# Hybrid decoder layer on one core: the last eight weight tiles are kept, and the second half of the tokens ends by column blocks

## The chip, the cores and the metric

The kernel runs on one core of one Trainium2 chip. The metric is the device time of one execution in microseconds. The time before is 1567.35 us, the median of 3 runs (1565.99 to 1568.28). The engines are named as the profile names them: PE is TensorE (matmuls), PEld its weight loads, DVE is VectorE, ACT is ScalarE, POOL is GpSimd and SP is SyncE. A name with q behind it is that engine's queue of issued DMAs.

## The reference

One decoder layer on 256 tokens of 2048 channels, all in float32. Two token mixers share one input projection and one output projection; then comes a gated MLP, and a final norm:

```
mixed = sigmoid(g_a) * y_a + sigmoid(g_b) * y_b
x = x + einsum('bsd,de->bse', mixed, w_out[l])
h = rmsnorm(x, norm_ffn_w[l])
gate, up = split(einsum('bsd,df->bsf', h, w_up[l]), 2, axis=-1)
gate = causal_dwconv(gate, conv_ffn_w[l]) + conv_ffn_b[l]
x = x + einsum('bsf,fd->bsd', gelu(gate) * up, w_down[l])
return rmsnorm(x, norm_final_w)
```

`rmsnorm(x, w)` is `x * rsqrt(mean(x * x) + 1e-6) * w`, one mean for each token. The MLP is 5632 wide, so `w_down` is 5632 x 2048. The change touches only the last two lines: the product with `w_down`, the residual add, the final norm and the write of the result.

## The kernel before

**Matmuls in three parts.** Every matmul of weights is done in a rounded float32 format. A weight tile is split into a high part (the rounded value) and a low part (what rounding left), and so are the activations. A product is three matmuls: high by high, low by high, high by low.

**The weight pipeline.** All weights come as 528 tiles (128 partitions x 1024 values, 512 KB) and two of another shape, in the fixed order of the list `srcs`. `fetch` (line 275) issues the load of a tile `raw` on SyncE's queue, into a ring of 4 buffers. `cast` (284) lets ScalarE write the high part `whi`, `split` (292) lets VectorE write the low part `wlo`, each into a ring of 4 buffers. So a load waits until the split of the tile four places earlier has freed its buffer, and a cast waits until TensorE is done with the tile four places earlier. `weights()` (317) hands out the next pair. A small model of the engines' times (`Plan`, and `pipeline` at 305) decides at which place of the program a fetch, cast or split is written, at most 3 tiles ahead of the one in use; what an engine then waits for, in program order, is settled on the chip.

**The product with `w_down`.** The activations stand in `hhi` and `hlo` (high and low part), the residual stream `x` in the tile `xt`. The result is 256 tokens x 2048 channels. It is accumulated in eight PSUM banks at once: two token halves t = 0, 1 of 128 tokens, by four column blocks c = 0 to 3 of 512 channels. `acc[c][t]` names them: for c = 0 and 1 they are tiles of their own (`psa`, t = 0, and `psb`, t = 1), for c = 2 and 3 both halves lie in one tile of two banks (`psm`). The rows of `w_down` are walked in 22 steps `kp` of 256 rows; each step has four weight tiles, one for each column block. `down_part(kp, c, t, hi, lo)` (1223) issues the six matmuls (two groups of 128 rows, three parts) of one tile for one token half. In the steps before the last, each tile is used for both halves in turn, 12 matmuls. In the last step (`LAST`, 1230) block 0 is done for both halves; then the loop over t takes blocks 1 to 3 of the first half, and ends that half, and then blocks 1 to 3 of the second half, and ends that one.

**How a half ends** (the loop over t, from line 1245). For each block, VectorE adds the PSUM bank to `xt`, and ScalarE squares the sum and sums it up by token (`sqj` is the square's scratch tile, `ssq5` the sums). VectorE reduces the four sums and scales them (`rs`), GpSimd raises to the power -0.5. VectorE multiplies blocks 2 and 3 by the norm's weights `nfin` meanwhile (called weighing below). Then blocks 0 and 1 are scaled and weighed in one VectorE operation, and blocks 2 and 3 are scaled by ScalarE. All four writes of a half are issued on SyncE's queue, in the order 0, 2, 1, 3. `nfin` was loaded in one broadcast load behind step 12, on ScalarE's queue.

Nearly every instruction is recorded through a helper, so the profile gives line 94 for all; they are told apart by their tiles.

Of the kernel before, what the change touches and what calls it, by code (L numbers as in the profile page):

```python
# [13 lines left out]
P = 128  # L14
# [93 lines left out]
def kernel(  # L108
# [35 lines left out]
    def nm(s):  # L144
        cnt[0] += 1
        return f"{s}_{cnt[0]}"
# [125 lines left out]
    def soon(eng, time):  # L272
        return time <= max(now["PE"], now[eng])

    def fetch():
        i = len(raws)
        src = srcs[i]
        raw = wpool.tile(list(src.shape), F32, tag="raw", name=nm("raw"), bufs=4)
        plan.at(free[i - 4] if i >= 4 else 0.0)
        nc.sync.dma_start(raw, src)  # L280
        landed.append(plan.ready)
        raws.append(raw)

    def cast():
        i = len(rounded)
        hi = wpool.tile(list(raws[i].shape), F32R, tag="whi", name=nm("whi"))
        plan.at(max(landed[i], now["PE"] if i > AHEAD else 0.0))
        nc.scalar.copy(hi, raws[i])
        cast_at.append(plan.ready)
        rounded.append(hi)  # L290

    def split():
        i = len(made)
        raw, hi = raws[i], rounded[i]
        plan.at(max(cast_at[i], now["PE"] if i > AHEAD else 0.0))
        if hi.shape[1] == 8:
            lo = None
            nc.vector.tensor_tensor(hi[:, :, 32:64], raw[:, :, 0:32], hi[:, :, 0:32].bitcast(F32), op=ALU.subtract)
        else:
            lo = wpool.tile(list(raw.shape), F32R, tag="wlo", name=nm("wlo"))  # L300
            nc.vector.tensor_tensor(lo, raw, hi.bitcast(F32), op=ALU.subtract)
        free.append(plan.ready)
        made.append((hi, lo))
# [923 lines left out]
            mm(acc[c][t], ll(k, t), hi[:, kk, :], start=False, stop=False)  # L1227
            mm(acc[c][t], lh(k, t), lo[:, kk, :], start=False, stop=(k == KF - 1))

    LAST = KF // 2 - 1  # L1230
    nfin = None
    for kp in range(LAST + 1):
        for c in range(4 if kp < LAST else 1):
            w = weights()
            for t in range(2):
                down_part(kp, c, t, *w)
# [1 line left out]
                    side()  # L1238
        if kp == 12:
            until(lambda: not threads)  # L1240
            nfin = big.tile([P, D], F32, tag="xhl", name="nfin")
            nc.scalar.dma_start(nfin, norm_final_w.partition_broadcast(P))
    ws = [weights() for c in range(3)]
    ssq5 = cpool.tile([P, 2, 4], F32, name="ssq5")
    for t in range(2):
        for c in range(1, 4):
            down_part(LAST, c, t, *ws[c - 1])
        for c in range(4):
            xs = xt[:, t, c * 512 : (c + 1) * 512]
            nc.vector.tensor_tensor(xs, xs, acc[c][t], op=ALU.add)  # L1250
            jk = cpool.tile([P, 512], F32, tag="sqj", name=nm("sqj"))
            nc.scalar.activation(jk, xs, AF.Square, accum_out=ssq5[:, t, c : c + 1])
        rs = cpool.tile([P, 1], F32, name=nm("rs"))
        nc.vector.tensor_reduce(rs, ssq5[:, t, :], axis=mybir.AxisListType.X, op=ALU.add)
        nc.vector.tensor_scalar(rs, rs, 1.0 / D, EPS, op0=ALU.mult, op1=ALU.add)
        nc.gpsimd.tensor_tensor(rs, rs, epsx[:, 0:1], op=ALU.pow)
        for c in (2, 3):
            xs = xt[:, t, c * 512 : (c + 1) * 512]
            nc.vector.tensor_tensor(xs, xs, nfin[:, c * 512 : (c + 1) * 512], op=ALU.mult)
        for c in (0, 2, 1, 3):  # L1260
            xs = xt[:, t, c * 512 : (c + 1) * 512]
            if c < 2:
                nc.vector.scalar_tensor_tensor(xs, xs, rs, nfin[:, c * 512 : (c + 1) * 512],
                                               op0=ALU.mult, op1=ALU.mult)
            else:
                nc.scalar.activation(xs, xs, AF.Copy, scale=rs)
            nc.sync.dma_start(out[0, t * P : (t + 1) * P, c * 512 : (c + 1) * 512], xs)


# [29 lines left out]
```

## Time and profile before

| What | Value |
|---|---|
| median of 3 runs | 1567.35 us (1565.99 to 1568.28) |
| the profiled execution's own time | 1567.87 us |
| its span | 1566.1 us |
| TensorE busy | 1540.2 us |
| VectorE busy | 1036.6 us |
| ScalarE busy | 787.2 us |
| mean granted TensorE clock | 0.994 |

A span runs from the first to the last event of the profile; the execution's own time is a little longer. In a row of a timeline the columns are: start in us from the span's start, duration in us, engine, line, operation, result and operands, shape, how many instructions are merged in the row, and in brackets the idle time before it with what ended it. A tile's row has minimum, median and maximum of the durations in ns. A row of loads or writes has the KB of each and the median us from issue to landing.

### The profile page before, as it was taken

What the parts mean: (1) busy time and instruction counts of PE and PEld (TensorE: products, weight loads), DVE (VectorE), ACT (ScalarE), POOL (GpSimd) and SP (SyncE); (2) the same over time, 40 slices, a digit from 0 to 9 for tenths busy, and PEclk for the clock granted to TensorE, in tenths of its full rate; (3) what the DMA queues carried; (4) which work ended last, traced back from release to release, by engine and by line L of the source; (5) the groups of instructions that cost most, each with busy time, mean ns of one, the idle gap of its engine ahead of it and who ended that gap; (6) DMA issues with size and microseconds to landing.
All of it is one profiled execution on the core that took longest, in us unless ns stands there. A gap on an engine that the chain in (4) does not pass through costs nothing.

```text
span 1566.1 us, 19803 instructions
## 1 busy us (share of the span) xinstructions
PE 1540.2 (98%) x7212; PEld 1261.8 (81%) x7212; DVE 1036.6 (66%) x1488; ACT 787.2 (50%) x1036; POOL 68.0 (4%) x109
## 2 busy tenths in 40 slices
PE   7999999999999999999999999999999999999996
PEld 5787788787878887888888888888888888888885
DVE  4778967788778766865565666666667666544444
ACT  6474574456545854454454445454454444433334
POOL 1201000100010001000000000000000000000000
PEclk9999999999999999999999999999999999999998
DMA  7887974788568857774756888888888887665663
GB/s 227 218 257 191 264 205 140 182 253 245 147 188 234 239 162 202 191 205 133 252 179 187 246 230 233 247 248 250 243 231 232 255 244 210 233 197 191 220 195 110
DMA packets 342585, 333.52 MB, mean 213 GB/s; under 512 B 181031, under 2 KB 201559, under 8 KB 342359
## 3 DMA queue, kind: packets, MB, share of 16 engines
q1 hardware_dynamic: 339776, 327.78, 72.0%
q10 hardware_dynamic: 2710, 4.48, 0.8%
q8 instruction: 56, 0.92, 0.2%
q14 instruction: 43, 0.34, 0.1%
HBM read 309.11 MB, written 23.10 MB: 212 GB/s over the span
## 4 chain that ended last, share of the span: by engine, by line
PE 92%; DVE 3%; DMA 2%; ACT 1%; SPq 1%; issue 1%; DVEq 0%; ACTq 0%
PE psm L94 79%; PE psa L94 8%; PE psb L94 5%; DMA raw<-in_w_in_dram 2%; DVE wlo L94 1%; DVE tmp L94 1%; SPq L94 1%; DVE tb L94 1%; ACT whi L94 0%; DVE xt L94 0%; DVE tn L94 0%; DMA x<-in_x_dram 0%; ACT sqj L94 0%; DVE cy L94 0%; ACT ev L94 0%
## 5 line engine op out<-in xcount | busy, mean ns | idle before, releaser
L94 DVE TENSOR_TENSOR wlo<-raw,whi 128x1024 fp32r<-128x1024 f32 x528 | 641.4, 1222 | 409.7 <-ACT whi L94 404.2
L94 ACT CAST whi<-raw 128x1024 fp32r<-128x1024 f32 x530 | 555.7, 1052 | 621.9 <-PE psm L94 452.2
L94 PE MATMUL psm<-whi,xhl 128*128 128x512 f32 x1792 | 566.8, 398 | 4.3 <-ACT whi L94 4.0
L94 PE MATMUL psm<-whi,fhl 128*128 128x512 f32 x1408 | 433.6, 389 | 0.0
L94 PEld LDWEIGHTS psm<-whi,xhl 128*128 128x128 f32 x1792 | 334.7, 190 | 75.3 <-ACT whi L94 5.1
L94 PE MATMUL psm<-wlo,xhl 128*128 128x512 f32 x896 | 352.7, 394 | 4.2 <-DVE wlo L94 4.2
L94 PEld LDWEIGHTS psm<-whi,fhl 128*128 128x128 f32 x1408 | 264.1, 188 | 54.9
L94 PE MATMUL psm<-wlo,fhl 128*128 128x512 f32 x704 | 273.9, 389 | 0.0
L94 PEld LDWEIGHTS psm<-wlo,xhl 128*128 128x128 f32 x896 | 169.6, 189 | 43.3 <-DVE wlo L94 7.0
L94 PEld LDWEIGHTS psm<-wlo,fhl 128*128 128x128 f32 x704 | 132.1, 188 | 27.4
L94 PE MATMUL psm<-whi,hhi 128*128 128x512 f32 x176 | 68.5, 389 | 0.0
L94 PE MATMUL psm<-whi,hlo 128*128 128x512 f32 x176 | 68.5, 389 | 0.0
L94 PE MATMUL psm<-wlo,hhi 128*128 128x512 f32 x176 | 68.5, 389 | 0.0
L94 ACT ACTIVATE fev<-psm,rs 128x512 f32<-128x512 f32 x44 | 27.9, 686 | 46.2 <-PE psm L94 46.2
L94 PE MATMUL psm<-whi,mhi 128*128 128x512 f32 x128 | 50.5, 394 | 0.0
L94 PE MATMUL psm<-wlo,mhi 128*128 128x512 f32 x128 | 50.0, 390 | 0.0
L94 PE MATMUL psm<-whi,mlo 128*128 128x512 f32 x128 | 49.9, 390 | 0.0
L94 DVE SCALAR_TENSOR_TENSOR cy<-kq,cqw,cy 128x255 f32<-128x255 f32 (+2 forms) x96 | 44.1, 479 | 1.6
L94 DVE SCALAR_TENSOR_TENSOR y<-gs,cfw,y 128x255 f32<-128x255 f32 x88 | 42.6, 484 | 3.1
L94 DVE TENSOR_TENSOR tmp<-lb,tb 128x248 f32<-128x248 f32 (+30 forms) x124 | 37.1, 299 | 4.7 <-DMA lb<-cdd 1.8
L94 DVE TENSOR_TENSOR tb<-tb,tmp 128x248 f32<-128x248 f32 (+30 forms) x124 | 37.3, 301 | 4.3
L94 DVE STREAM_TRANSPOSE tn<-fev 128x1024 f32<-128x1024 f32 x22 | 27.3, 1242 | 17.1 <-ACT fev L94 15.2
(194 smaller groups left out, 1238.2 us busy)
## 6 DMA issues: line engine op xcount, KB each, us to landing
raw<-in_w_in_dram SPq DMA_DIRECT2D x226, 512.0 KB, 4.6
raw<-in_w_up_dram SPq DMA_DIRECT2D x176, 512.0 KB, 4.9
raw<-in_w_down_dram SPq DMA_DIRECT2D x88, 512.0 KB, 4.5
flip<-tn SPq DMA_DIRECT2D x136, 128.0 KB, 3.3
raw<-in_w_out_dram SPq DMA_DIRECT2D x32, 512.0 KB, 4.3
gs<-flip SPq DMA_DIRECT2D x11, 512.0 KB, 5.9
us<-flip SPq DMA_DIRECT2D x11, 512.0 KB, 6.6
kq<-flip SPq DMA_DIRECT2D x8, 512.0 KB, 6.4
```

The source lines that it names most:

```text
L94: r = getattr(self.eng, op)(out, *args, **kw)
```

## The change

The last two steps of `w_down` (eight tiles, `KEPT = 2` steps) are used for the first token half only, as they come, and kept. The first four of the eight are written into a new tile `last` (high and low parts beside each other) in place of the rings; it takes the place in SBUF where `nfin` stood. The other four stay in the rings of `whi` and `wlo`. Then the second half's matmuls follow by column block: `turn(c)` issues the 12 matmuls of the two kept tiles of block c.

The end of a half is cut into pieces: `added` (add and square), `weighed`, and `finish` (reduce, power, scaling, writes). They are written between the blocks: the first half's adds ahead of the second half's block 0, its `finish` behind the add of the second half's block 0, and the adds of the second half's blocks each behind its own matmuls. In `finish`, ScalarE scales blocks 0 and 1 and issues their writes itself; VectorE scales block 2 (weighed before) and scales and weighs block 3, and SyncE issues these two. `nfin` is two tiles of two blocks each, loaded by two loads into the buffers of two tiles of the MLP that are no longer used (`gs`, `y`).

```diff
--- before.py
+++ after.py
@@ -272,6 +272,13 @@
     def soon(eng, time):
         return time <= max(now["PE"], now[eng])
 
+    KEPT = 2
+    last = []
+
+    def keep(i):
+        j = i - (len(srcs) - 4 * KEPT)
+        return last[0][:, j] if 0 <= j < 4 * KEPT - 4 else None
+
     def fetch():
         i = len(raws)
         src = srcs[i]
@@ -283,7 +290,8 @@
 
     def cast():
         i = len(rounded)
-        hi = wpool.tile(list(raws[i].shape), F32R, tag="whi", name=nm("whi"))
+        hi = keep(i)
+        hi = wpool.tile(list(raws[i].shape), F32R, tag="whi", name=nm("whi")) if hi is None else hi[:, 0]
         plan.at(max(landed[i], now["PE"] if i > AHEAD else 0.0))
         nc.scalar.copy(hi, raws[i])
         cast_at.append(plan.ready)
@@ -297,7 +305,8 @@
             lo = None
             nc.vector.tensor_tensor(hi[:, :, 32:64], raw[:, :, 0:32], hi[:, :, 0:32].bitcast(F32), op=ALU.subtract)
         else:
-            lo = wpool.tile(list(raw.shape), F32R, tag="wlo", name=nm("wlo"))
+            lo = keep(i)
+            lo = wpool.tile(list(raw.shape), F32R, tag="wlo", name=nm("wlo")) if lo is None else lo[:, 1]
             nc.vector.tensor_tensor(lo, raw, hi.bitcast(F32), op=ALU.subtract)
         free.append(plan.ready)
         made.append((hi, lo))
@@ -1227,10 +1236,12 @@
             mm(acc[c][t], ll(k, t), hi[:, kk, :], start=False, stop=False)
             mm(acc[c][t], lh(k, t), lo[:, kk, :], start=False, stop=(k == KF - 1))
 
-    LAST = KF // 2 - 1
-    nfin = None
-    for kp in range(LAST + 1):
-        for c in range(4 if kp < LAST else 1):
+
+
+    ROWS = KF // 2
+    nfin = []
+    for kp in range(ROWS - KEPT):
+        for c in range(4):
             w = weights()
             for t in range(2):
                 down_part(kp, c, t, *w)
@@ -1238,33 +1249,69 @@
                     side()
         if kp == 12:
             until(lambda: not threads)
-            nfin = big.tile([P, D], F32, tag="xhl", name="nfin")
-            nc.scalar.dma_start(nfin, norm_final_w.partition_broadcast(P))
-    ws = [weights() for c in range(3)]
+            last.append(big.tile([P, 4, 2, 2, 512], F32R, tag="xhl", name="last"))
+            for n, tag in enumerate(("gs", "y")):
+                nfin.append(fp.tile([P, 2, 512], F32, tag=tag, name=f"nfin{n}"))
+                nc.scalar.dma_start(nfin[n].rearrange("p c d -> p (c d)"),
+                                    norm_final_w[n * 1024 : (n + 1) * 1024].partition_broadcast(P))
+    kept = []
+    for kp in range(ROWS - KEPT, ROWS):
+        for c in range(4):
+            kept.append((kp, c, *weights()))
+            down_part(kp, c, 0, *kept[-1][2:])
+            side()
     ssq5 = cpool.tile([P, 2, 4], F32, name="ssq5")
-    for t in range(2):
-        for c in range(1, 4):
-            down_part(LAST, c, t, *ws[c - 1])
-        for c in range(4):
-            xs = xt[:, t, c * 512 : (c + 1) * 512]
-            nc.vector.tensor_tensor(xs, xs, acc[c][t], op=ALU.add)
-            jk = cpool.tile([P, 512], F32, tag="sqj", name=nm("sqj"))
-            nc.scalar.activation(jk, xs, AF.Square, accum_out=ssq5[:, t, c : c + 1])
+
+    def added(t, c):
+        xs = xt[:, t, c * 512 : (c + 1) * 512]
+        nc.vector.tensor_tensor(xs, xs, acc[c][t], op=ALU.add)
+        jk = cpool.tile([P, 512], F32, tag="sqj", name=nm("sqj"))
+        nc.scalar.activation(jk, xs, AF.Square, accum_out=ssq5[:, t, c : c + 1])
+
+    def weighed(t, c):
+        xs = xt[:, t, c * 512 : (c + 1) * 512]
+        nc.vector.tensor_tensor(xs, xs, nfin[c // 2][:, c % 2], op=ALU.mult)
+
+    def finish(t):
         rs = cpool.tile([P, 1], F32, name=nm("rs"))
         nc.vector.tensor_reduce(rs, ssq5[:, t, :], axis=mybir.AxisListType.X, op=ALU.add)
         nc.vector.tensor_scalar(rs, rs, 1.0 / D, EPS, op0=ALU.mult, op1=ALU.add)
         nc.gpsimd.tensor_tensor(rs, rs, epsx[:, 0:1], op=ALU.pow)
-        for c in (2, 3):
+        weighed(t, 2)
+        for c in (3, 0, 2, 1):
             xs = xt[:, t, c * 512 : (c + 1) * 512]
-            nc.vector.tensor_tensor(xs, xs, nfin[:, c * 512 : (c + 1) * 512], op=ALU.mult)
-        for c in (0, 2, 1, 3):
-            xs = xt[:, t, c * 512 : (c + 1) * 512]
-            if c < 2:
-                nc.vector.scalar_tensor_tensor(xs, xs, rs, nfin[:, c * 512 : (c + 1) * 512],
-                                               op0=ALU.mult, op1=ALU.mult)
+            to = out[0, t * P : (t + 1) * P, c * 512 : (c + 1) * 512]
+            if c in (0, 1):
+                nc.scalar.activation(xs, xs, AF.Copy, scale=rs)
+                nc.scalar.dma_start(to, xs)
+            elif c == 2:
+                nc.vector.tensor_scalar(xs, xs, rs, None, op0=ALU.mult)
+                nc.sync.dma_start(to, xs)
             else:
-                nc.scalar.activation(xs, xs, AF.Copy, scale=rs)
-            nc.sync.dma_start(out[0, t * P : (t + 1) * P, c * 512 : (c + 1) * 512], xs)
+                nc.vector.scalar_tensor_tensor(xs, xs, rs, nfin[1][:, 1], op0=ALU.mult, op1=ALU.mult)
+                nc.sync.dma_start(to, xs)
+
+    def turn(c):
+        for kp, cc, hi, lo in kept:
+            if cc == c:
+                down_part(kp, c, 1, hi, lo)
+
+    for c in range(4):
+        added(0, c)
+    turn(0)
+    for c in range(2):
+        weighed(0, c)
+    turn(1)
+    added(1, 0)
+    finish(0)
+    turn(2)
+    weighed(1, 0)
+    added(1, 1)
+    turn(3)
+    weighed(1, 1)
+    added(1, 2)
+    added(1, 3)
+    finish(1)
 
 
 # ---- launch: one core; inputs and outputs as the reference has them ----
```

On VectorE the end of the program reads as follows, in the kernel before, from the first half's reduce on (`psb_10878`, `psb_10880`, `psm_10881` and `psm_10882` are the accumulators of the second half's blocks 0 to 3, `rs` the factor of the tokens):

```order
L94 TENSOR_REDUCE rs_12462<-ssq_12431 128x1
L94 TENSOR_SCALAR rs_12462<-rs_12462 128x1
L94 TENSOR_TENSOR xt<-xt,nfin 128x512 x2
L94 SCALAR_TENSOR_TENSOR xt<-xt,rs_12462,nfin 128x512 x2
L94 TENSOR_TENSOR xt<-xt,psb_10878 128x512
L94 TENSOR_TENSOR xt<-xt,psb_10880 128x512
L94 TENSOR_TENSOR xt<-xt,psm_10881 128x512
L94 TENSOR_TENSOR xt<-xt,psm_10882 128x512
L94 TENSOR_REDUCE rs_12506<-ssq_12431 128x1
L94 TENSOR_SCALAR rs_12506<-rs_12506 128x1
L94 TENSOR_TENSOR xt<-xt,nfin 128x512 x2
L94 SCALAR_TENSOR_TENSOR xt<-xt,rs_12506,nfin 128x512 x2
```

And in the changed kernel, from the add of the second half's block 0 on, after four adds and two weighings of the first half:

```order
L94 TENSOR_TENSOR xt<-xt,psb_10878 128x512
L94 TENSOR_REDUCE rs_12456<-ssq_12414 128x1
L94 TENSOR_SCALAR rs_12456<-rs_12456 128x1
L94 TENSOR_TENSOR xt<-xt,nfin_11844 128x512
L94 SCALAR_TENSOR_TENSOR xt<-xt,rs_12456,nfin_11844 128x512
L94 TENSOR_SCALAR xt<-xt,rs_12456 128x512
L94 TENSOR_TENSOR xt<-xt,nfin_11842 128x512
L94 TENSOR_TENSOR xt<-xt,psb_10880 128x512
L94 TENSOR_TENSOR xt<-xt,nfin_11842 128x512
L94 TENSOR_TENSOR xt<-xt,psm_10881 128x512
L94 TENSOR_TENSOR xt<-xt,psm_10882 128x512
L94 TENSOR_REDUCE rs_12504<-ssq_12414 128x1
```

Before, all four adds of the second half stand behind the first half's scaling; now the first stands ahead of the first half's reduce, and the other three between its scaling and the second half's reduce, with two weighings between them. Behind the second half's reduce one weighing is left of two.

On ScalarE the end of the program before, from the last square of the first half on (`sqj` is the square of a block):

```order
L94 ACTIVATE sqj_12460,ssq_12431<-xt 128x512
L94 ACTIVATE xt<-xt,rs_12462 128x512 x2
L94 ACTIVATE sqj_12495,ssq_12431<-xt 128x512
L94 ACTIVATE sqj_12498,ssq_12431<-xt 128x512
L94 ACTIVATE sqj_12501,ssq_12431<-xt 128x512
L94 ACTIVATE sqj_12504,ssq_12431<-xt 128x512
L94 ACTIVATE xt<-xt,rs_12506 128x512 x2
```

And now, from the square of the second half's block 0 on:

```order
L94 ACTIVATE sqj_12454,ssq_12414<-xt 128x512
L94 ACTIVATE xt<-xt,rs_12456 128x512
L94 DMA out_dram<-xt 128x512
L94 ACTIVATE xt<-xt,rs_12456 128x512
L94 DMA out_dram<-xt 128x512
L94 ACTIVATE sqj_12483,ssq_12414<-xt 128x512
L94 ACTIVATE sqj_12499,ssq_12414<-xt 128x512
L94 ACTIVATE sqj_12502,ssq_12414<-xt 128x512
L94 ACTIVATE xt<-xt,rs_12504 128x512
L94 DMA out_dram<-xt 128x512
L94 ACTIVATE xt<-xt,rs_12504 128x512
L94 DMA out_dram<-xt 128x512
```

Before, the two scalings of the first half stood ahead of four squares; now one square stands ahead of them, three behind, and each scaling has its write behind it in ScalarE's own program.

## The prediction

> **What bounds the kernel now.** I read the page first, then the chain of waits over the last 26 us, then the timelines of each engine there, and last the DMA view of the final writes. Page:
>
> ```profile
> span 1566.1 us, 19803 instructions
> PE 1540.2 (98%) x7212; PEld 1261.8 (81%) x7212; DVE 1036.6 (66%) x1488; ACT 787.2 (50%) x1036; POOL 68.0 (4%) x109
> GB/s 227 218 257 191 264 205 140 182 253 245 147 188 234 239 162 202 191 205 133 252 179 187 246 230 233 247 248 250 243 231 232 255 244 210 233 197 191 220 195 110
> PE 92%; DVE 3%; DMA 2%; ACT 1%; SPq 1%; issue 1%; DVEq 0%; ACTq 0%
> ```
>
> TensorE is busy 98% of the span. The change removes no matmul, so what it can win is where TensorE has stopped. The end, from TensorE's timeline:
>
> ```profile
> 1549.89 0.39 PE L94 MATMUL psm<-wlo,hhi 128*128 128x512 f32 x1
> 1550.12 0.39 PE L94 MATMUL psb<-whi,hhi 128*128 128x512 f32 x1
> ...
> 1553.97 0.39 PE L94 MATMUL psm<-wlo,hhi 128*128 128x512 f32 x1
> ```
>
> The first row ends the first token half (1549.89 + 0.39 = 1550.28), the last row ends the second (1554.36). Between the second and third row lie 17 steps, so one matmul takes (1553.97 - 1550.12) / 17 = 0.227 us, six of them (one weight tile, one token half) 1.36. After 1554.36 come 11.74 us without TensorE. What they hold, in the timelines of VectorE, ScalarE, GpSimd and SyncE:
>
> ```profile
> 1550.32 0.69 DVE L94 TENSOR_TENSOR xt<-xt,psm 128x512 f32<-128x512 f32 x1 [0.67 <-PE psm L94]
> 1551.86 0.16 DVE L94 TENSOR_REDUCE rs<-ssq 128x1 f32<-128x4 f32 x1 [0.85 <-ACT sqj L94]
> 1553.32 1.41 DVE L94 SCALAR_TENSOR_TENSOR xt<-xt,rs,nfin 128x512 f32<-128x512 f32 x2
> 1554.64 1.28 DVE L94 TENSOR_TENSOR xt<-xt,psb 128x512 f32<-128x512 f32 x2
> 1555.84 1.28 DVE L94 TENSOR_TENSOR xt<-xt,psm 128x512 f32<-128x512 f32 x2
> 1558.43 0.16 DVE L94 TENSOR_REDUCE rs<-ssq 128x1 f32<-128x4 f32 x1 [1.32 <-ACT sqj L94]
> 1558.70 1.28 DVE L94 TENSOR_TENSOR xt<-xt,nfin 128x512 f32<-128x512 f32 x2
> 1559.90 1.41 DVE L94 SCALAR_TENSOR_TENSOR xt<-xt,rs,nfin 128x512 f32<-128x512 f32 x2
> ```
> ```profile
> 1551.10 0.63 ACT L94 ACTIVATE sqj<-xt 128x512 f32<-128x512 f32 x1 [0.64 <-DVE xt L94]
> 1553.24 1.33 ACT L94 ACTIVATE xt<-xt,rs 128x512 f32<-128x512 f32 x2 [1.42 <-POOL rs L94]
> 1555.42 0.63 ACT L94 ACTIVATE sqj<-xt 128x512 f32<-128x512 f32 x1 [0.84 <-DVE xt L94]
> 1559.83 1.33 ACT L94 ACTIVATE xt<-xt,rs 128x512 f32<-128x512 f32 x2 [1.42 <-POOL rs L94]
> ```
> ```profile
> 1552.28 0.93 POOL L94 TENSOR_TENSOR rs<-rs,epsx 128x1 f32<-128x1 f32 x1 [706.38 <-DVE rs L94]
> 1558.86 0.93 POOL L94 TENSOR_TENSOR rs<-rs,epsx 128x1 f32<-128x1 f32 x1 [5.66 <-DVE rs L94]
> ```
> ```profile
> 1554.09 0.36 SPq L94 DMA_DIRECT2D out_dram<-xt  x1
> 1560.67 1.79 SPq L94 DMA_DIRECT2D out_dram<-xt  x4
> ```
>
> The first half shows the chain as it is when three of the four adds and squares are done before TensorE stops: end 1550.28, add 1550.32, square 1551.10, reduce 1551.86, power 1552.28, scaling 1553.24, first write issued 1554.09, which is 3.81 us after its last matmul. The second half does all four adds and four squares after its last matmul, because VectorE takes them in program order behind the first half's scaling: adds from 1554.64, squares from 1555.42, reduce only at 1558.43, first write 1560.67, which is 6.31 us after 1554.36. The difference, 2.50 us, is work that was waiting in line.
>
> Behind the first write stand 1566.1 - 1560.67 = 5.43 us. From the DMA view of 1554 to 1567 (a column is 0.325 us) and the output's rows:
>
> ```profile
> GB/s 0 0 44 334 391 378 397 328 328 385 328 303 13 0 0 0 0 0 0 0 0 0 0 328 397 359 384 353 328 397 340 315 25 0 0 0 0 0 0 0
> out_dram<-xt SPq DMA_DIRECT2D x8, 256.0 KB, 2.9
> ```
>
> The second burst fills nine columns without a gap: 4 x 262,144 bytes in 2.93 us is 358 GB/s. These writes are bound by their bytes, not by the four issues.
>
> **The change part by part.**
>
> *Second half by column blocks.* TensorE's count stays, so its end stays 1554.36 if it is fed. Counting back 12 matmuls (2.72 us) each: the second half's block 0 ends 1546.20, block 1 1548.92, block 2 1551.64, block 3 1554.36, and the first half is complete at 1543.48. VectorE's new scaling by the norm's factor alone has only a half-size row:
>
> ```profile
> L94 DVE TENSOR_SCALAR y<-gs,cfw,vec 128x256 f32<-128x256 f32 x44 | 17.9, 408 | 0.3 <-DMA gs<-flip 0.3
> ```
>
> It takes between that 0.41 and the 0.75 of a scaling with weights (half of 1.41 and a little); I take 0.75. With the durations above (an add or a weighing 0.69), VectorE adds the four first-half blocks as they come (last one 1543.5 to 1544.2), weighs two, adds block 0 of the second half at 1546.24 to 1546.93, and reduces at 1546.95. Power ends near 1548.3, the first half's scaling on VectorE near 1549.8. Then weigh, add block 1 (1550.45 to 1551.13), wait for its square, weigh (to 1552.55), add block 2 (to 1553.25). Block 3's add is free to start at 1554.40. So one add and one square remain after the end, the first half's 3.81 us chain. That is the gain of 2.50. VectorE also has one weighing instead of two under the power: before, its scaling started at 1553.32 though ScalarE's started at 1553.24, so another 0.08. Sum: 2.58.
>
> *ScalarE scales blocks 0 and 1 and issues their writes.* In the first half this lies before the square of block 1 on ScalarE, and block 1's weighing, block 2's add and square queue behind that. The nearest rows of an issue, for ScalarE and for SyncE:
>
> ```profile
> L94 ACTq DMA_DIRECT2D xt<-in_x_dram x4: 388/492/517, 758.9 to 760.3; - x4
> L94 SPq DMA_DIRECT2D out_dram<-xt x8: 332/401/458, 1554.1 to 1562.1; - x8
> ```
> ```profile
> xt<-in_x_dram ACTq DMA_DIRECT2D x4, 512.0 KB, 8.1
> ```
>
> At 0.33 to 0.52 each, ScalarE scales from 1548.34, issues, scales, issues, and is free near 1550.85, before block 1's add ends at 1551.13. I take the upper row and cost it at nothing; the cover is 1.1 us (1553.25 to 1554.40), and beyond that each microsecond costs one. In the last step ScalarE scales, issues, scales, issues: its second write is issued about 1.1 us after its first, when over half of the 2.93 us burst is still ahead. Cost nothing, bounds 0 and -0.3 (next section).
>
> [...]
>
> *TensorE's last eight tiles, first half only.* Tiles 80 to 87 are now used up in 1.36 us each instead of 2.72, and twice the weights must be there. How they come now:
>
> ```profile
> 1524.25 1.05 ACT L94 CAST whi<-raw 128x1024 fp32r<-128x1024 f32 x1 [1.67 <-PE psb L94]
> ...
> 1543.29 1.05 ACT L94 CAST whi<-raw 128x1024 fp32r<-128x1024 f32 x1 [1.67 <-PE psm L94]
> ```
> ```profile
> 1525.34 1.22 DVE L94 TENSOR_TENSOR wlo<-raw,whi 128x1024 fp32r<-128x1024 f32 x1 [1.49 <-ACT whi L94]
> ```
> ```profile
> 1526.59 8.53 SPq L94 DMA_DIRECT2D raw<-in_w_down_dram  x4
> ```
> ```profile
> raw<-in_w_down_dram SPq DMA_DIRECT2D x4, 512.0 KB, 4.4
> ```
>
> The two casts are those of tiles 80 and 87, seven steps of 2.72 apart. Each waits for TensorE to leave a buffer, 8.2 us ahead of use, so TensorE reaches tile 80 at 1532.4, and in the new order tile 87 at 1532.4 + 7 x 1.36 = 1541.9 (its low part at 1542.4). A raw tile is fetched when the split four tiles earlier ends (1525.34 + 1.22, issue at 1526.59). At the old pace the last raw would be issued at 1526.59 + 8.53 - 0.37 = 1534.75 (0.37 being about one issue), land 4.4 later at 1539.15, be cast and split in 2.35, ready at 1541.5: still 0.9 early. In the new order casts 80 to 83 have buffers of their own and wait for nothing but their data, and casts 84 to 87 find ring buffers that TensorE left before 1532.4. Following landing, cast and split tile by tile, the last raw is issued near 1530.6 and ready near 1537.4, 4.6 us early. Cost: nothing.
>
> *The final norm's weights in two loads, and a VectorE scaling in place of a ScalarE one.* Before, the one load stands here:
>
> ```profile
> L94 ACTq DMA_DIRECT2D nfin<-in_norm_final_w_dram x1: 346/346/346, 1453.5 to 1453.5; - x1
> ```
>
> That is 90 us before use, and two issues fit into the 1.67 us that ScalarE idles between casts. The scaling lies inside the write burst. Nothing.
>
> Sum: 2.58 us. The profiled execution took 1567.87 us, 1.77 more than its span, and would take 1565.29. The median shown is 1567.35 (runs 1565.99 to 1568.28), so the forecast is 1567.35 - 2.58 = 1564.8. That is 0.16%; about 0.2% (3.13 us) is what a measurement of this kernel can tell from no change.
>
> **The rivals.**
>
> *A: two queues also shorten the burst.* If ScalarE's row beside SyncE's keeps the DMA engines at the best column above, 397 GB/s, the 1.05 MB take 2.64 us instead of 2.93; the last issue also comes some 0.3 us sooner after the first (1.1 against 1.4 from the first issue to the fourth). Together or alone 0.3 to 0.6: 1564.2 to 1564.5, at the edge of 0.2%. Against it: the single queue shows no gap. [...]
>
> *B: ScalarE is held by its own writes.* If an issue kept ScalarE until the write has landed (2.9 us, twice), the square of block 1 would come 4.8 us later than counted, 3.7 past the cover, and the gain is gone: 1568.5, more if the last writes wait so too. Half of that hold leaves about 1566. Against it: the four loads of `xt` were issued from ScalarE within 1.4 us (758.9 to 760.3), while they took 8.1 to land (median).
>
> *C: TensorE starves on the last eight tiles (slower).* Place: tiles 84 to 87. If raws land one after another every x us from raw 83's landing at 1528.3 (issued one step of 2.72 before 1526.59, plus 4.4), the last low part is ready at 1528.3 + 4x + 2.3 and is needed at 1542.4. It stalls from x = 2.95, eats the gain at 3.6, and is slower by 0.2% from 4.4, the full time to landing: 5.8 us late, 1570.6. Against it: the page's 264 GB/s over a slice of 39 us is 1.99 us for a tile of 524,288 bytes.
>
> *D: it does not do what it says.* TensorE's blocks 2 and 3 of the second half write the other half of a tile that VectorE reads; if that made them wait for the first half's scaling (near 1549.8) instead of its adds, block 2 (from 1548.92) would start 0.9 late: 1565.7.
>
> **How the numbers follow.** Forecast 0.61, A 0.18, B 0.12, C 0.04, D 0.05. The median of a few runs adds some 0.8 us either way (the three runs lie -1.36 and +0.93 around theirs). Lower end: A's 1564.2 less 0.8, about 1563.4. Upper end: half of B or D with the same scatter, 1567.0. Faster by over 0.2% means below 1564.2: a quarter of the forecast's chance (0.15) and over half of A's (0.10), so 0.25. Slower by over 0.2%: C and a part of B, 0.05. Within: 0.70.
>
> **What would show it.** In the changed profile: TensorE without a gap up to its last matmul; one add and one square behind it; reduce about 1.6 us and the first write about 3.7 us after it; a last burst of about 2.9 us at 358 GB/s. The forecast is wrong if TensorE shows idle time waiting for a `last` or `wlo` tile, if block 2's add ends after block 3's last matmul, or if the stretch from the first write to the end is not about 5.4 us.

## The result, and the profile after

| What | Before | After |
|---|---|---|
| median, runs of the same chip | 1568.19 us (15 runs, 1564.98 to 1569.31) | 1564.55 us (15 runs, 1561.81 to 1567.36) |
| the profiled execution's own time | 1567.87 us | 1562.02 us |
| its span | 1566.1 us | 1560.3 us |
| end of the last matmul | 1554.36 us | 1551.19 us |
| from there to the end (the tail; spans finer than the page prints them) | 11.77 us | 9.08 us |

The ratio after to before is 0.9979, 95% interval 0.9971 to 0.9986: 3.3 us less, between 2.2 and 4.5 (the two medians themselves lie 3.64 apart). The forecast gain of 2.58 us lies inside. The profiled executions differ by more, some 5.8 us, and the table says where: 2.69 us behind the last matmul, 3.17 us ahead of it. The first part is the change. The second part needs an explanation of its own, since the change issues the same instructions in the first 1450 us.

The page of the kernel after, its span, its engines and the shares of the chain of waits:

```profile
span 1560.3 us, 19797 instructions
PE 1537.2 (99%) x7212; PEld 1259.7 (81%) x7212; DVE 1037.2 (66%) x1490; ACT 787.1 (50%) x1036; POOL 68.4 (4%) x109
PE 93%; DVE 3%; DMA 1%; ACT 1%; issue 1%; SPq 0%; POOLq 0%; POOL 0%; ACTq 0%; DVEq 0%
```

TensorE's instructions are as many as before. The end, from the timelines of TensorE, VectorE, ScalarE and GpSimd of the kernel after:

```profile
1550.80 0.39 PE L94 MATMUL psm<-wlo,hhi 128*128 128x512 f32 x1
1545.05 0.75 DVE L94 SCALAR_TENSOR_TENSOR xt<-xt,rs,nfin 128x512 f32<-128x512 f32 x1 [0.44 <-POOL rs L94]
1545.72 0.48 DVE L94 TENSOR_SCALAR xt<-xt,rs 128x512 f32<-128x512 f32 x1
1546.72 0.68 DVE L94 TENSOR_TENSOR xt<-xt,psb 128x512 f32<-128x512 f32 x1
1548.80 0.68 DVE L94 TENSOR_TENSOR xt<-xt,psm 128x512 f32<-128x512 f32 x1
1551.22 0.69 DVE L94 TENSOR_TENSOR xt<-xt,psm 128x512 f32<-128x512 f32 x1 [1.75 <-PE psm L94]
1552.76 0.16 DVE L94 TENSOR_REDUCE rs<-ssq 128x1 f32<-128x4 f32 x1 [0.85 <-ACT sqj L94]
1546.98 0.35 ACTq L94 DMA_DIRECT2D out_dram<-xt  x1
1547.43 0.63 ACT L94 ACTIVATE sqj<-xt 128x512 f32<-128x512 f32 x1 [0.48 <-DVE xt L94]
1552.01 0.63 ACT L94 ACTIVATE sqj<-xt 128x512 f32<-128x512 f32 x1 [1.71 <-DVE xt L94]
1554.90 0.37 ACTq L94 DMA_DIRECT2D out_dram<-xt  x1
1555.32 0.72 ACT L94 ACTIVATE xt<-xt,rs 128x512 f32<-128x512 f32 x1 [0.45 <-ACT xt L94]
1553.18 0.93 POOL L94 TENSOR_TENSOR rs<-rs,epsx 128x1 f32<-128x1 f32 x1 [8.16 <-DVE rs L94]
```

The row that decides is the add at 1551.22 with [1.75 <-PE psm]: VectorE has idled 1.75 us and waits for TensorE's last block. Before, that add stood behind the first half's scaling and three other adds. One add (1551.22), one square (1552.01), the reduce (1552.76), the power (1553.18), a scaling, and the first write is issued at 1554.90, 3.71 us after the last matmul, where before it took 6.31. From 1554.90 to the end (1560.27, one digit finer than the page) are 5.37 us, where before it took 5.46 (1560.67 to 1566.13; with the page's 1566.1 these are the prediction's 5.43). So of the 2.69 us, 2.60 lie ahead of the first write and 0.09 behind it. The writes, from the DMA view of 1548 to 1561 of the kernel after (a column is 0.325 us):

```profile
GB/s 372 372 372 391 170 0 0 0 0 0 0 0 0 0 0 0 0 0 0 0 0 0 0 44 372 384 372 391 385 391 353 378 158 0 0 0 0 0 0 0
```

The first half's burst is over at the left edge, long before the second's begins. The last burst has no gap.

**Ahead of the last matmul.** GpSimd's few instructions are milestones of a program that is the same in both kernels up to there: the first norm factor, and two later ones. Before, then after:

```profile
37.55 0.84 POOL L94 TENSOR_TENSOR rs<-ms,epsx 128x2 f32<-128x2 f32 x1 [31.66 <-DVE ms L94]
260.20 1.63 POOL L94 TENSOR_TENSOR ro<-ro,epsx 128x8 f32<-128x8 f32 x1 [66.55 <-DVE ro L94]
845.17 0.73 POOL L94 TENSOR_TENSOR rs<-ms,epsx 128x2 f32<-128x2 f32 x1 [107.84 <-DVE ms L94]
```
```profile
35.97 0.85 POOL L94 TENSOR_TENSOR rs<-ms,epsx 128x2 f32<-128x2 f32 x1 [30.05 <-DVE ms L94]
257.04 1.64 POOL L94 TENSOR_TENSOR ro<-ro,epsx 128x8 f32<-128x8 f32 x1 [65.66 <-DVE ro L94]
842.00 0.73 POOL L94 TENSOR_TENSOR rs<-ms,epsx 128x2 f32<-128x2 f32 x1 [107.84 <-DVE ms L94]
```

The kernel after is 1.58 us ahead at the first, 3.16 at the second, 3.17 at the third and at its last matmul. So the second part arises at two places in the first 260 us, about 1.6 us at each. What differs there is the granted clock. Windows of 1 us near 17 us and of 2 us near 170 us, before (columns: window, length and busy time with instructions of the five engines, then the granted clock, DMA share and GB/s):

```profile
17.00:18.00 1.00, 0.78 (x2) 0.30 (x2) 0.94 (x2) 1.00 (x2) 0.00 (x0) 0.74 0.00 0
18.00:19.00 1.00, 0.77 (x2) 0.50 (x2) 1.00 (x2) 0.97 (x4) 0.00 (x0) 0.50 0.00 0
19.00:20.00 1.00, 1.00 (x4) 0.73 (x3) 0.56 (x1) 0.97 (x3) 0.00 (x0) 0.50 0.61 49
20.00:21.00 1.00, 1.00 (x4) 0.81 (x3) 0.00 (x0) 0.96 (x4) 0.00 (x0) 0.56 0.79 279
168.00:170.00 2.00, 1.70 (x4) 1.41 (x5) 2.00 (x3) 0.85 (x1) 0.00 (x0) 0.50 0.97 274
170.00:172.00 2.00, 2.00 (x6) 1.52 (x6) 1.97 (x4) 2.00 (x9) 0.00 (x0) 0.50 1.00 254
172.00:174.00 2.00, 2.00 (x6) 1.53 (x5) 1.83 (x6) 2.00 (x6) 0.00 (x0) 0.50 0.80 264
```

The same of the kernel after:

```profile
18.00:19.00 1.00, 1.00 (x4) 0.85 (x5) 1.00 (x1) 0.97 (x4) 0.00 (x0) 1.00 0.10 10
166.00:168.00 2.00, 1.58 (x4) 1.29 (x5) 2.00 (x3) 0.65 (x1) 0.00 (x0) 0.68 1.07 281
168.00:170.00 2.00, 2.00 (x6) 1.57 (x5) 2.00 (x3) 2.00 (x9) 0.00 (x0) 0.50 0.84 244
170.00:172.00 2.00, 2.00 (x10) 1.58 (x9) 1.79 (x7) 2.00 (x7) 0.00 (x0) 0.96 0.88 262
```

Before, TensorE ran at half clock near 18 us for 0.52 + 1 + 1 + 0.88 = 3.4 us (twice the missing share of each window), and near 170 us for 6 us and, at 0.92 and 0.88 in the windows on either side of those shown, for 0.32 and 0.48 us more, 6.8 us in all, twice that. After, it did so near 168 us for one such stretch only (1.28 + 2 + 0.16 = 3.4 us), and not near 18 us. In the kernel before, TensorE's matmuls stood 0.43 us apart in these stretches (from 168.90 to 174.02 twelve of them, 5.12 us) and 0.23 behind them; busy throughout, it would lose half of 3.4 us, 1.7 us, in each (an estimate). Two stretches fewer are 3.4 us, about the 3.17 found. Whether that has to do with the change, the experiments tell.

### The profile page after: what moved, and what is told of

Its sections match the earlier page's. It is cut to its first block, busy times and chain, and to the rows that moved or that the text cites. A ratio compares the mean times of both kernels' runs of the same rounds, so it can differ in the third digit from the quotient of the medians.

```text
span 1560.3 us, 19797 instructions
## 1 busy us (share of the span) xinstructions
PE 1537.2 (99%) x7212; PEld 1259.7 (81%) x7212; DVE 1037.2 (66%) x1490; ACT 787.1 (50%) x1036; POOL 68.4 (4%) x109
## 4 chain that ended last, share of the span: by engine, by line
PE 93%; DVE 3%; DMA 1%; ACT 1%; issue 1%; SPq 0%; POOLq 0%; POOL 0%; ACTq 0%; DVEq 0%
PE psm L94 80%; PE psa L94 8%; PE psb L94 5%; DMA raw<-in_w_in_dram 1%; DVE wlo L94 1%; DVE tmp L94 1%; DVE tb L94 1%; ACT whi L94 1%; SPq L94 0%; DMA x<-in_x_dram 0%; ACT ev L94 0%; ACT xhl L94 0%; DVE tn L94 0%; ACT xt L94 0%; POOLq L1341 0%
## 5 line engine op out<-in xcount | busy, mean ns | idle before, releaser
L94 DVE TENSOR_TENSOR tmp<-lb,tb 128x248 f32<-128x248 f32 (+30 forms) x124 | 37.1, 299 | 4.3 <-DMA lb<-cdd 1.4
```

The lines of the kernel that those rows point to most:

```text
L94: r = getattr(self.eng, op)(out, *args, **kw)
```

## The experiments

Theory: the gain is the work that stood in line behind the last matmul, and the 3.17 us ahead of it are scatter from one execution to the next. Rivals: the gain lies ahead of the end; the two queues shorten the burst (A); ScalarE is held by its writes (B); TensorE's supply is near its limit (C); the column blocks, or the order on VectorE alone, are what matters. Tails below are read as in the table.

**1. The kernel after once more**, unchanged.

> The changed kernel once more. My theory (the gain is the work that stood in line on VectorE behind TensorE's last matmul, nothing else): 9.1 us from the end of the last matmul to the span's end, against 11.74 before, whatever the time of the last matmul; the time of the last matmul moves in steps of about 1.6 us between executions of one and the same kernel, one step for each 3.4 us stretch in which TensorE was granted half its clock (three such stretches before the last matmul in the profile of before, one in that of after). Rival (the change itself makes TensorE end 3.2 us earlier): the last matmul ends near 1551.2 again with one such stretch, and the total is 5.8 us below the kernel before.

Measured: 1564.81 us (12 runs), before 1566.99 (35 runs), ratio 0.9986 (0.9977 to 0.9994). The page's span and the last matmul:

```profile
span 1562.4 us, 19797 instructions
...
1552.93 0.39 PE L94 MATMUL psm<-wlo,hhi 128*128 128x512 f32 x1
```

The tail is 9.10 us again. The last matmul ends at 1553.32, 2.1 us later than in the first profile of the same kernel; the first norm factor comes at 37.69 us in place of 35.97, and the mean granted clock is 0.996 in place of 0.998. What lies ahead of the last matmul goes with the execution, not with the kernel.

**2. The second half's kept tiles in row order**, VectorE's order as in the change.

```diff
-    def turn(c):
-        for kp, cc, hi, lo in kept:
-            if cc == c:
-                down_part(kp, c, 1, hi, lo)
+    def turn(n):
+        for kp, c, hi, lo in kept[2 * n : 2 * n + 2]:
+            down_part(kp, c, 1, hi, lo)
...
     turn(1)
+    turn(2)
     added(1, 0)
     finish(0)
-    turn(2)
```

> The second half's matmuls of the eight kept tiles in the order of the rows (all four blocks of one step, then of the other) in place of column blocks; VectorE's and ScalarE's programs stay word for word in the same order. So block 0 of the second half is complete only 4.1 us before the end, and the first half's reduce stands behind its add. My theory (what counts is the place in VectorE's line): block 1's square comes at +0.55 us after the last matmul, reduce at +4.15 instead of +1.6, 11.7 us from last matmul to end, all the gain lost. Rival (the gain is that the first half is out of the way and TensorE covers it): 9.1 us as in the changed kernel.

Measured: 1566.35 us, ratio 0.9997 (0.9987 to 1.0006); the tail is 11.48 us. VectorE's timeline, with the last matmul ending at 1553.06:

```profile
1549.01 0.69 DVE L94 TENSOR_TENSOR xt<-xt,psb 128x512 f32<-128x512 f32 x1 [4.91 <-PE psb L94]
...
1554.75 1.28 DVE L94 TENSOR_TENSOR xt<-xt,psm 128x512 f32<-128x512 f32 x2
```

VectorE waits 4.91 us for the second half's block 0, with the first half's end queued behind it, and the last two adds begin 1.69 us after TensorE has stopped. Nearly the whole gain is gone, with the same matmuls, bytes and kept tiles.

**3. Row order, but the first half ended ahead of the second half's adds** (`turn` as in 2).

```diff
...
-    turn(1)
-    added(1, 0)
     finish(0)
+    turn(1)
     turn(2)
-    weighed(1, 0)
+    added(1, 0)
     added(1, 1)
+    weighed(1, 0)
     turn(3)
-    weighed(1, 1)
     added(1, 2)
+    weighed(1, 1)
     added(1, 3)
     finish(1)
```

> Matmuls in the order of the rows as in the run beside it, but VectorE and ScalarE end the first half (reduce, power, scaling, writes) ahead of the second half's first add, and the second half's adds stand ahead of the weighings that wait for their squares. My theory: block 3's add starts at most 0.15 us late, 9.1 to 9.4 us from last matmul to end; the column blocks themselves are worth nothing. Rival (column blocks are needed so that a half can end in pieces): 10.5 us or more.

Measured: 1564.45 us, ratio 0.9984 (0.9975 to 0.9992); the tail is 9.09 us. VectorE's last add, with the last matmul ending at 1551.87:

```profile
1551.90 0.69 DVE L94 TENSOR_TENSOR xt<-xt,psm 128x512 f32<-128x512 f32 x1
```

It begins 0.03 us behind TensorE. So the column blocks themselves are not needed: in row order the blocks are complete 1.36 us apart instead of 2.72, and that is enough if VectorE has nothing else in line.

**4. One step kept instead of two.**

```diff
-    KEPT = 2
+    KEPT = 1
```

> Four kept tiles (one step of w_down) instead of eight, the order otherwise as in the changed kernel: 5.4 us of the second half's matmuls to cover the first half's end, instead of 10.9. My theory (VectorE's work in line is what counts, and the cover of 1.1 us that I counted is what is left of the 10.9): the first half's scaling ends at about the last matmul, block 1's square near +1.0, block 3's add ends near +3.6, reduce near +4.8, and 12.3 us from the last matmul to the end, 0.5 slower than before. Rival (any kept tiles will do): 9.1 us.

Measured: 1568.84 us, ratio 1.0008 (0.9999 to 1.0016); the tail is 11.93 us. VectorE, with the last matmul ending at 1556.98:

```profile
1557.03 0.68 DVE L94 TENSOR_TENSOR xt<-xt,psb 128x512 f32<-128x512 f32 x1
...
1559.10 1.28 DVE L94 TENSOR_TENSOR xt<-xt,psm 128x512 f32<-128x512 f32 x2
```

Three adds are left behind the end. With four tiles the second half lasts 5.4 us. The first half's end, with the add of block 0 in it and the wait of its scaling for its power, keeps VectorE until 1556.51, a weighing follows, and the add of block 1 begins only at 1557.03. The second kept step buys the time, not a better order.

**5. The kernel before, with the end reordered on VectorE, ScalarE and GpSimd alone**, no tiles kept: both halves' adds first, both factors, then all scalings and writes.

```diff
...
+        if t == 0:
+            for c in range(4):
+                added(0, c)
+            added(1, 0)
+            rs0 = factor(0)
+    added(1, 1)
+    added(1, 2)
+    weighed(0, 2)
+    added(1, 3)
+    weighed(0, 3)
+    rs1 = factor(1)
+    scaled(0, rs0)
+    weighed(1, 2)
+    weighed(1, 3)
+    scaled(1, rs1)
```

> The kernel before, TensorE's program unchanged and no tile kept; only VectorE, ScalarE and GpSimd are reordered: the second half's four adds and squares and both factors stand ahead of the first half's scaling. All writes on SyncE. My theory (the adds waiting in line cost 2.5 us, but the first half's scaling, 1.4 us on each engine, its two weighings and its 1 MB of writes must go somewhere, and behind the last matmul is only the place where they were not before): first write of the second half 4.9 to 5.5 us after the last matmul, its burst queued behind the first half's, 10.6 to 11.4 us from the last matmul to the end (11.77 before, 9.1 after). Rival (the order on VectorE is all, the kept tiles are not needed): 9.1 us.

Measured: 1566.53 us, before 1568.13 (33 runs), ratio 0.9994 (0.9984 to 1.0004); the tail is 11.06 us. VectorE's reduce and the DMA view of 1552 to 1565, with the last matmul ending at 1553.75:

```profile
1555.32 0.16 DVE L94 TENSOR_REDUCE rs<-ssq 128x1 f32<-128x4 f32 x1 [0.25 <-ACT sqj L94]
```
```profile
GB/s 0 0 0 0 0 0 0 0 0 0 0 0 0 0 0 0 340 397 378 378 328 328 385 359 378 372 258 277 315 378 397 397 403 296 88 0 0 0 0 0
```

The reduce comes 1.57 us behind the last matmul, exactly as in the kernel after, so the line on VectorE is gone here too. Yet only 0.7 of the 2.69 us is won: now both halves write at the end, 19 columns instead of 10. A line of work has become a line of bytes. Keeping tiles is what lets the first half's 1.05 MB leave under the second half's matmuls.

**6. All writes issued by SyncE** (rival A, and B).

```diff
                 nc.scalar.activation(xs, xs, AF.Copy, scale=rs)
-                nc.scalar.dma_start(to, xs)
+                nc.sync.dma_start(to, xs)
```

> The changed kernel with all writes issued by SyncE, ScalarE scaling as it does. My theory: the last burst is bound by its bytes, so who issues is worth nothing, 9.0 to 9.3 us from the last matmul to the end. Rival A (two queues move the burst faster): 9.4 to 9.7 us.

Measured: 1565.81 us, ratio 0.9985 (0.9975 to 0.9995); the tail is 9.15 us, 0.07 more than with two issuers. The DMA view of 1552 to 1565:

```profile
GB/s 334 397 309 372 57 0 0 0 0 0 0 0 0 0 0 0 0 0 0 0 0 0 0 321 391 340 397 359 340 391 321 328 38 0 0 0 0 0 0 0
```

The eight full columns behind the first have a mean of 358 GB/s with one issuer, and 378 in the row of the kernel after with two (382 over the seven full columns in the profile of 1, 359 in the last burst of the kernel before). So with two issuers the bytes moved faster here, which rival A had; but of some 0.15 us over a burst only 0.07 arrives at the end.

**7. The second half writes 64 of its 128 tokens.**

```diff
+            to, part = (to[:64], xs[:64]) if t else (to, xs)
...
-                nc.scalar.dma_start(to, xs)
+                nc.scalar.dma_start(to, part)
...
```

> The changed kernel, but the second half's four writes carry only the first 64 of its 128 tokens (the other 64 rows of the result are left unwritten), in rows of the same 2 KB. My theory (the last burst is bound by its bytes, 358 to 380 GB/s): half of 2.8 us falls away, 7.6 to 7.9 us from the last matmul to the end. Rival (the end is set by the issues and the fixed time to landing): 8.8 to 9.1 us.

Measured: 1565.2 us, ratio 0.9983 (0.9974 to 0.9993); the tail is 8.90 us. The DMA view of 1553 to 1566:

```profile
GB/s 366 397 385 378 309 0 0 0 0 0 0 0 0 0 0 0 0 0 0 0 0 0 0 0 0 170 202 195 170 196 208 202 202 70 0 0 0 0 0 0
```

Half the bytes took as long as all: the writes from 64 partitions ran at 170 to 208 GB/s in this run, where the first half's, from 128, show 366 to 397 at the left of the same row. The expected cut of over a microsecond did not come, for a reason that has nothing to do with the question. It decides nothing about the burst.

**8. The second half writes 256 of each block's 512 channels**, from all 128 partitions, to put that question again.

```diff
+            to, part = (to[:, :256], xs[:, :256]) if t else (to, xs)
...
```

> The changed kernel, but the second half's four writes carry only the first 256 of each block's 512 columns, for all 128 tokens (the other columns of these rows are left unwritten). The run that wrote 64 of 128 tokens ran its burst at 176 to 206 GB/s, so it halved the rate with the bytes and did not decide. My theory (the burst is bound by its bytes when all partitions take part): the burst runs at 330 GB/s or more, 7.7 to 8.3 us from the last matmul to the end. Rival (issues and the fixed time to landing set the end): 8.8 to 9.1 us again.

Measured: 1563.02 us (7 runs), before 1567.65 (20 runs), ratio 0.9971 (0.9960 to 0.9981); the tail is 7.68 us. The DMA view of 1549 to 1562:

```profile
GB/s 0 63 384 397 384 359 378 391 397 365 107 0 0 0 0 0 0 0 0 0 0 0 0 0 0 0 0 0 0 63 350 344 331 331 196 0 0 0 0 0
```

The tail is 1.40 us shorter, and 524,288 bytes at 378 GB/s are 1.39 us. The burst is bound by its bytes, as the prediction had it.

**9. The last two kept tiles loaded twice** (rival C: how much slack has TensorE's supply?). The second load of a tile goes into the same buffer and follows the first.

```diff
-        nc.sync.dma_start(raw, src)
+        for _ in range(2 if i >= len(srcs) - 2 else 1):
+            nc.sync.dma_start(raw, src)
```

> The changed kernel with the last two of the eight kept tiles loaded twice in a row into the same buffer, each load waiting for the one before, so that the last tile comes some 8.8 us later (two more loads of 4.4 us). My theory: the weights of the last tile are ready about 5 us before TensorE needs them, so TensorE waits 3.3 to 4.3 us there, and the end after the last matmul is 9.1 us as before. Rival (TensorE is near starving there as it is): a wait of 7 us or more.

Measured: 1568.55 us, ratio 1.0005 (0.9995 to 1.0015); the tail is 9.19 us. TensorE at the last kept tile, and the landing times of the raw tiles from 1520 to 1545:

```profile
1541.98 0.50 PE L94 MATMUL psm<-whi,hhi 128*128 128x512 f32 x1 [1.81 <-ACT whi L94]
...
1543.25 0.50 PE L94 MATMUL psm<-wlo,hhi 128*128 128x512 f32 x1 [0.53 <-DVE wlo L94]
```
```profile
DMA to landing us min/median/max: 3.7/4.7/6.4
```

TensorE now waits 1.81 + 0.53 = 2.34 us, less than expected. If the two extra loads took the shortest time in that row, 3.7 us each, the slack was 2 x 3.7 - 2.3 = 5.1 us (an estimate; longer loads would mean more). In the kernel after, the trace shows it directly: VectorE's last split, and TensorE's first use of it:

```profile
1533.17 1.23 DVE L94 TENSOR_TENSOR wlo<-raw,whi 128x1024 fp32r<-128x1024 f32 x1 [0.28 <-ACT whi L94]
...
1539.24 0.39 PE L94 MATMUL psm<-wlo,hhi 128*128 128x512 f32 x1
```

1539.24 - 1534.40 = 4.8 us early. Rival C would need a supply at least that much later.

**10. Eight matmuls more behind the first weight tile**, to keep TensorE busy near 17 us. They read the tile again and write a PSUM block that nothing reads.

```diff
             hi, lo = weights()
...
+            if fill is not None and c == 0:
+                for _ in range(8):
+                    tc.nc.tensor.matmul(fill, lh(0, 0), hi[:, 0, :], start=True, stop=True)
```

> The changed kernel with eight more matmuls on TensorE behind the first weight tile, into a PSUM bank that nothing reads, recorded outside the model of times so that every other instruction stays where it is: they fill 1.8 us of the stretch near 15 us in which TensorE waits for the second tile. My theory (a half-clock stretch follows a stretch in which TensorE was idle for a large part; this is where the 1.6 us steps between executions of one kernel come from): no half-clock stretch near 17 to 19 us, the first factor of the mixer's norm on GpSimd at 35.8 to 36.1 us as in the profiles without that stretch, 9.1 us from the last matmul to the end, and a median 0.5 to 1.5 us below the changed kernel's. Rival (the stretches come by themselves): the stretch near 17 us in some executions as before, the same median, or slower by what the eight matmuls take.

Measured: 1566.34 us (11 runs, 1565.23 to 1567.72), ratio 0.9994 (0.9985 to 1.0003). TensorE's timeline:

```profile
15.18 2.39 PE L353 MATMUL psm<-whi,xhl 128*128 128x512 f32 x8
17.41 0.60 PE L94 MATMUL psb<-ident,x 128*128 128x128 f32 x4
19.87 0.73 PE L94 MATMUL psm<-whi,xhl 128*128 128x512 f32 x2 [1.86 <-ACT whi L94]
```

The runs lie closer together, and the profile has no half clock near 18 us. (That need not hold for the other executions: 8 of the 11 have a mean clock of 0.996, as the profile of the kernel after in 12 has with two stretches, from 18.2 and from 168.4 us.) But the median is about 1.5 us above those of the kernel after in its three sets of runs (1564.55, 1564.81 and, below, 1565.16). The row of 19.87 says why: the wait of 1.86 us is not covered, it has moved. The cast that TensorE waits for stands on ScalarE behind the evictions of the transposes of 17.41, and the added matmuls delayed these.

**11. Seven matmuls more, behind these transposes**, and **12. the kernel after a third time** beside it.

```diff
...
+            if fill is not None and c == 1:
+                for _ in range(7):
+                    tc.nc.tensor.matmul(fill, lh(0, 0), hi[:, 0, :], start=True, stop=True)
             plan.at(0.0)
             hi, lo = weights()
```

> The kernel after with seven matmuls more (128x128 by 128x512, into a psum block that nothing reads yet), placed behind the second weight tile's transposes (the first fill stood ahead of them), where TensorE waits 1.86 us for the high part of that tile. Seven by 0.227 us are 1.6 us, so they should end before the cast does and delay nothing: the wait named above shrinks to about 0.3 us and the low part's to about 0.5 us. Theory (the idle there is what starts the stretch of half clock near 17 us, and the stretch is what puts executions 1.6 us apart): no stretch between 17 and 21 us, the first norm factor near 36.0 us, the tail 9.1 us, a scatter of 2 to 3 us in place of 5, and a median 0.5 to 1.0 us below the kernel after, near 1564.0. Rival (the stretches come at times of their own, whatever idles): a stretch can still stand there, and the median is the kernel after's within 0.3 us. A median above the kernel after's by over 1 us would mean that the added matmuls cost something by themselves.

> The kernel after, once more, unchanged, as the one to compare with on the same chip in the same minutes: 1564.5 to 1565, tail 9.1 us, a ratio to the kernel before of 0.998 to 0.9985.

Measured: 1563.95 us (11 runs, 1562.28 to 1564.97), ratio 0.9976 (0.9968 to 0.9985); the kernel after 1565.16 us (12 runs, 1563.56 to 1567.67), ratio 0.9989 (0.9981 to 0.9998). TensorE's timeline and a window of the kernel with seven more:

```profile
15.69 1.86 PE L343 MATMUL psm<-whi,xhl 128*128 128x512 f32 x7
17.80 0.73 PE L94 MATMUL psm<-whi,xhl 128*128 128x512 f32 x2 [0.26 <-ACT whi L94]
19.06 0.50 PE L94 MATMUL psm<-wlo,xhl 128*128 128x512 f32 x1 [0.52 <-DVE wlo L94]
```
```profile
18.00:19.00 1.00, 0.54 (x2) 0.10 (x1) 1.00 (x2) 1.00 (x2) 0.00 (x0) 1.00 0.00 0
```

The wait is filled, the clock stays at 1.00 though TensorE still idles almost half of that window, and the median is 1.2 us below the kernel after's. Drawing from both sets of runs again and again puts that difference between 0.3 and 3.3 us (95%). All 11 executions have a mean clock of 0.997 or 0.998; of the 12 of the kernel after, none is above 0.996. So with the idle of 1.86 us filled the half clock near 18 us stayed away in this profile (with the idle there, it comes in some executions and not in others, as the last section tells), and the median fell with it. Not all went as expected: the first norm factor came at 37.03 us, not near 36, since this execution's transposes already stood at 15.13 us, where the first profile of the kernel after has them at 14.27. A matmul ahead of the transposes shows why, in the kernel after and then here:

```profile
13.35 0.39 PE L94 MATMUL psm<-wlo,xhl 128*128 128x512 f32 x1
```
```profile
14.71 0.63 PE L94 MATMUL psm<-wlo,xhl 128*128 128x512 f32 x1
```

TensorE began at half rate in both, its matmuls 0.43 us apart where later they are 0.23 apart. In the kernel after this ended at 13.1 us, here only at 15.5 (the clock column of a window there shows 1.00 all the same). The tail is 9.10 us. This is the lowest median of a kernel here that leaves nothing out, and what it adds is independent of the change. Single executions of the kernel after do better without it: in the first set, 7 of 15 have a mean clock of 0.997 or 0.998, and they take 1561.81 to 1563.03 us.

## Why the prediction was right, point by point

- **The gain of 2.58 us is the line behind TensorE's end: right, 2.60 measured up to the first write, and 0.09 more behind it.** It came as forecast: one add and one square left, the reduce 1.57 us after the last matmul (1.6 forecast), the first write 3.71 us after it (3.7). All kernels with that order of VectorE and the tiles kept have a tail of 9.1 to 9.2 us (seven profiles); undoing the order (2) or one kept step (4) brings 11.5 to 11.9 back.
- **5.43 us behind the first write: right, 5.37.** Bytes bound it: half of them save 1.40 us (8). The burst was forecast at 358 GB/s and ran at 378.
- **ScalarE's issues cost nothing: right, but the margin was thinner than counted in one place and wider in another.** ScalarE was to be free 0.28 us before block 1's add ended; it was free at 1547.33 and the add ended at 1547.40, 0.07 us. The cover before the last add was to be 1.1 us and is 1.75. One reason is a price: the scaling by the factor alone takes 0.48 us, near the lower of its two bounds, not the 0.75 taken.
- **TensorE's supply costs nothing: right.** 4.8 us early instead of 4.6, and a supply some 7 us later costs 2.3 (9).
- **Rivals.** A: two issuers did shorten the burst (378 against 358 GB/s), but were worth 0.07 us at the end, not 0.3 to 0.6 (6). B: ScalarE's next instruction began 0.05 us after an issue (1554.90 + 0.37, then 1555.32), so it was not held. C and D: TensorE has no gap in its last 30 us; a window from 1521.00 to 1551.19 has it busy for 30.18 of 30.19 us.
- **The time: 1564.8 forecast, 1564.55 measured.** That it came so close is in part luck: the kernel before stood at 1568.19 beside it, 0.84 above the median that the forecast started from, and the medians lie 3.64 apart, 1.06 more than the gain forecast. The three comparisons of the same kernel give gains of 0.21%, 0.14% and 0.11%: 3.3, 2.2 and 1.7 us, and 2.6 lies inside all three intervals (2.2 to 4.5, 0.9 to 3.6, 0.3 to 3.0). The first lies just past the bound of 0.2%, on the side to which the prediction gave 0.25; the other two lie within it. The prediction's scatter of 0.8 us "either way" for a median of few runs covers that; what the scatter is made of it did not know.

## What to carry to other kernels

When an engine's end is followed by a fixed chain, look at what the engines of that chain still have in line at that moment, in program order: work that could have been done earlier costs its full length there. Moving that work is not enough if its writes then meet the last ones (5): the earlier half must end early enough for its bytes to leave, too. And a single profile of a kernel with 0.3% of scatter overstates or hides a gain of this size; a milestone that both programs share tells how much of a difference lies ahead of the change.

## What the runs showed of the hardware that was not expected

- **The half clock came in stretches of 3.4 us, and TensorE had not been idle for all of the time ahead of them.** The kernel before has one stretch, from 17.48 us, and two on end from 167.66 in its profile; the kernel after has none near 18 us and one from 166.7, and one from 18.2 and one from 168.4 when it was profiled again in 12. In the two profiles that have both, the stretch near 168 us starts 150.2 us after the one near 18. TensorE's half rate at the start ended, by the spacing of its matmuls, at 14.1 us in the kernel before, at 13.1 and 14.8 in these two profiles of the kernel after, at 15.5 in 11 and at 16.0 in 10. TensorE was busy for about 45% of the 3.4 us ahead of the stretch near 18 us in both profiles that have it. Of the 3.4 us behind the half rate it was busy for 52% in the first profile of the kernel after, 59% in 10 and about 80% in 11, and no stretch came next. Ahead of the stretch near 168 us it was busy for 21% of 3.4 us in the kernel before and for 9% in the kernel after. What decides was not tried: no run varied this share by itself beyond 10 and 11, and a matmul's end is modelled.
- **The same idle went with a half clock in one execution and not in another, and the first 40 us moved with it.** The idle of 1.86 us near 16 us is in all three profiles without added matmuls whose clock there is known. In the first of the kernel after the half rate ended at 13.1 us, no stretch follows, and the first norm factor comes at 35.97 us; in the kernel before and in 12 it ended at 14.1 and 14.8, a stretch follows, and the factor comes at 37.55 and 38.02. Of eleven profiles without added matmuls (all but that of 8), four have this factor at 35.8 to 36.1 us (the first of the kernel after, 2, 3 and 9), and seven at 37.1 to 38.7.
- **In 7, the writes from 64 partitions ran at about half the rate of those from 128** (170 to 208 against 366 to 397 GB/s, in one row). Why was not tried.
